# Attention step of a one-core hybrid layer: order of transposes, scores and fillers on TensorE

## The chip, the core and the metric

The kernel runs on one core of one Trainium2 chip. The metric is the device time of one execution in microseconds (us). Before the change it is 689.45 us, the median of 3 runs (689.14 to 689.67).

## The reference

The layer computes, for 1024 tokens of width 1024 (batch 1, one layer, float32):

```python
u = layer_norm(x) * (1 + scale) + shift          # scale, shift, gate from silu(c) @ w_ada + b_ada
fq, fk, fv, fg, ff, sq, sk, sv, sg = split(u @ w_in)
# 8 heads of 64, forgetting attention: causal softmax of q k / 8 + f_cum[query] - f_cum[key]
# 8 heads of 64, stick-breaking: sigmoid(z) times the product of sigmoid(-z) over the later keys
y = concat([fox * silu(fg), stick * silu(sg)]) @ w_out
out = layer_norm(2 ** 0.25 * x + gate * y, ln_g, ln_b)
```

## The kernel before, in words

**Number format.** Most products are done in three matmuls of float32r: each operand is split into a rounded high part and a low rest, and high x high, low x high and high x low are accumulated in PSUM. `m_step` (L292) is one such triple for a block of 128 input rows and 512 tokens.

**Pairs and units.** The 16 heads are handled as 8 pairs p; pairs 0 to 3 are the stick-breaking heads, 4 to 7 the forgetting ones. A unit (p, h, i) is one head h of a pair and one block i of 128 queries, with (i+1)*128 keys. There are 128 units, in an order that `order` (L1010) gives: i rises for the first four pairs, falls for the next three, and the last pair goes by query blocks from the last to the first.

**The steps of a unit.**
- `att_scores` (L445): the score matmuls S (L457, L458) into the only score tile; then for the stick-breaking heads two sigmoids on ACT (L479, L481), a running product on DVE (L486, L490) and a product on POOL (L492); for the forgetting heads a sum with minimum on DVE (L465), an exponential on ACT (L470), a reciprocal on DVE (L471) and a scaling on POOL (L473). The DVE instruction L465 is ordered behind the latest low part of the transposes (the list `lows`).
- `att_query` (L426): ACT copies the next unit's query block (L431).
- `att_transpose` (L497): TensorE transposes the weights, 128 columns at a time, in groups of up to four into one of two PSUM tiles T (L509); ACT copies a group as the high part (L511), DVE makes the low part (L512). Once a pair of query blocks is complete, its value product `att_pv` (L519, matmuls L526) is issued after the first group of the next unit's transposes; ACT, DVE and POOL then form the gated output (L533 to L536), which goes to DRAM.

**Fillers.** The projections of later pairs are not a stage of their own. They are written as generators whose pieces (six matmuls as a rule, and some pieces without any) are put between the attention's instructions. `fill(want)` (L1005) runs pieces until a count is reached, and the list `want` spreads `FILL[p]` pieces over the 16 units of pair p in half steps. `gen_last_g` (L969) is the last filler: the gate projection of pair 7, on two accumulators, with a load of the output weights of one pair (`load_wo`, L845) after each piece. In pair 7 its pieces are spread over the first `G7` units. The accumulators have two buffers (tag acc). After that the output projection's pieces (`tail`, `o_step` L888) fill in, `TAIL` pieces per step, from unit 116 on.

**What sets the order.** TensorE's instructions run in the order in which the program writes them (a manual schedule from L138 to the end). The other engines' queues are ordered by a planner from the program; `after(...)` puts instructions behind named ones of the same engine. The softmax work of unit k has a lag of `LAG` = 2 steps: step k of the loop at L1036 issues the scores of unit k and the transposes of unit k-2. `HELD` names the steps at which parts of pair 0's projections, held in SBUF, are evacuated (`evac_m`, L313).

Step k of the loop before the change, on TensorE: scores of unit k; first filler piece; transposes of unit k-2 with the value product that is ready; second filler piece; output pieces where it is their turn.

Of the kernel before, what the change touches and what calls it, by code (L numbers as in the profile page):

```python
# [16 lines left out]
NB = 8  # L17
# [10 lines left out]
def tile_hybrid_layer(  # L28
# [30 lines left out]
    def pt_tile(name, dt=F32R, shape=None):  # L59
        return big("pt", 3, name, dt, shape or [P, 2, 1024])  # L60

    def acc_tile(name):
        return ps.tile([P, 512], F32, tag="acc", bufs=2, name=name)

    def pv_tile(name, which=0):
        return ps.tile([P, 512], F32, tag=f"pv{which}", bufs=1, name=name)

    def t_tile(name):
        return ps.tile([P, 512], F32, tag="T", bufs=2, name=name)
# [13 lines left out]
    def after(*instructions):  # L83
        stack = ExitStack()
        for i in instructions:
            stack.enter_context(tc.issue_after(i.ins))
        return stack
# [177 lines left out]
    def evac_q(p, ch, acc, qst, heads):  # L265
        s = slice(ch * 512, ch * 512 + 512)
        for h in heads:
            r = slice(h * HD, h * HD + HD)
            o = slice((1 - h) * HD, (1 - h) * HD + HD)
            nc.scalar.activation(qst[h][r, s], acc[r, :], AF.Copy, scale=SCALE)  # L270
            nc.vector.scalar_tensor_tensor(qst[h][o, s], acc[r, :], SCALE, qst[h].bitcast(F32)[r, s],
                                           op0=ALU.mult, op1=ALU.subtract)
# [14 lines left out]
    def evac_g(p, ch, acc, sg):  # L287
        s = slice(ch * 512, ch * 512 + 512)
        nc.scalar.activation(sg[:, s], acc, AF.Tanh, scale=0.5)
        nc.vector.scalar_tensor_tensor(sg[:, s], sg[:, s], 1.0, acc, op0=ALU.add, op1=ALU.mult)  # L290
# [22 lines left out]
    def evac_m(p, m, ch, acc, heads=(0, 1)):  # L313
        if m == 0:
            evac_q(p, ch, acc, qst[p], heads)
        elif m == 1:
            return evac_k(p, ch, acc, kst[p], klo[p], heads)
        else:
            evac_g(p, ch, acc, sgt[p])
# [113 lines left out]
    masks, scaled, lows = [], [], []  # L433

    def att_causal(u):
        p, h, i = u
        if p >= 4:
            if not masks:
                masks.append(pv_tile("causal_ps", 1)[:, :P])
                nc.vector.tensor_copy(masks[0], causal)  # L440
            f = fb[2 * (p - 4) + h]
            dg = slice(i * P, i * P + P)
            nc.vector.tensor_tensor(f[:, dg], f[:, dg], masks[0], op=ALU.add)
# [53 lines left out]
    def att_transpose(u, between=()):  # L497
        p, h, i = u
        a = st_w.pop(u)
        j, qo = i // 2, (i % 2) * P  # L500
        for g in range((i // 4) + 1):
            n = min(4, i + 1 - 4 * g)
            if (p, h, j, g) not in st_pt:
                st_pt[p, h, j, g] = pt_tile(f"pt_{p}_{h}_{j}_{g}", F32R, [P, 2, 4, 256])
            hi, lo = (st_pt[p, h, j, g][:, x] for x in range(2))
            tp = t_tile(f"T_{p}_{h}_{i}_{g}")
            for b in range(n):
                kb = 4 * g + b
                nc.tensor.transpose(tp[:, b * P:(b + 1) * P], a[:, kb * P:(kb + 1) * P], ident)  # L509
            t3 = tp[:, :n * P].rearrange("p (a b) -> p a b", a=n)  # L510
            nc.scalar.copy(hi[:, :n, qo:qo + P], t3)  # L511
            lows[:] = [nc.vector.tensor_tensor(lo[:, :n, qo:qo + P], t3, hi.bitcast(F32)[:, :n, qo:qo + P],  # L512
                                               op=ALU.subtract)]
            while between:
                att_pv(*between.pop(0))
# [281 lines left out]
    for kb in range(NB):  # L797
# [9 lines left out]
        if kb < len(evacs):  # L807
            n, h = evacs[kb]
# [4 lines left out]
    held = att_tile("st_held")  # L813
# [31 lines left out]
    def load_wo(pr):  # L845
        hi = big(f"u{pr}", 1, f"woh_{pr}", F32R)
        lo = big(f"v{pr}", 1, f"wol_{pr}", F32R)
        nc.sync.dma_start(hi.bitcast(F32), wo_dr[0, pr])
        nc.sync.dma_start(lo.bitcast(F32), wo_dr[1, pr])
        wo[pr] = (hi, lo)  # L850
# [118 lines left out]
    def gen_last_g(p):  # L969
        tiles = fetch_m(p, 2)  # L970
        yield
        make_g(p)
        accs = [acc_tile(f"m_{p}_2_{ch}") for ch in range(2)]
        for kt in range(NB):
            for ch in (1, 0):
                m_step(accs[ch], tiles, kt, ch)
            if kt == NB - 1:
                for ch in (1, 0):
                    evac_m(p, 2, ch, accs[ch])
            load_wo(kt)  # L980
            yield

    fillers = chain([
# [10 lines left out]
    LEAD = 2  # L994
    LAG = 2
    W0 = 100.0
    OUT0 = 4
    TAIL = (2, 2, 2, 2, 2, 2, 4, 4, 4, 4, 8)
    G7 = 6
    HELD = {4: (1, 1), 5: (0, 0), 6: (1, 0), 10: (0, 1)}  # L1000
    FIRST_UNITS = 5
    YLOAD = (6, 9, 12, 14, 16)
# [2 lines left out]
    def fill(want):  # L1005
        while done[0] < want:
            done[0] += 1
            next(fillers, None)
# [10 lines left out]
    units = [u for p in range(NPAIR) for u in order(p)]  # L1019
    want = [0.0]  # L1020
    for p in range(NPAIR):
# [3 lines left out]
        if p == NPAIR - 1:  # L1025
            size = [1] * G7 + [0] * (16 - G7)
        for w in size:
# [3 lines left out]
    seen = set()  # L1031
    ready = []
    LAST = 16 * (NPAIR - 1)
    tail = chain([gen_out_first(6), gen_out_last(6)] + [gen_out(t) for t in OUT_ORDER[1:]])
    fill(2)
    for k in range(len(units) + LAG + 1):  # L1036
        if k < len(units):
            if k == 16 * 4 - 1:
                load_fb(0)
                load_fb(1)  # L1040
            if k == 0:
                att_query(units[0])
            issued = att_scores(units[k], units[k + 1] if k + 1 < len(units) else None)
            if k == 16 * 4 - 1:
                att_causal(units[k + 1])
            if k + 1 < len(units):
                att_query(units[k + 1])
            p, h, i = units[k]
            if 4 <= p < NPAIR - 1 and i == 0:
                load_fb(2 * (p - 4) + h + 2)  # L1050
        fill(want[2 * k + LEAD + 1])
        if LAG <= k < len(units) + LAG:
            u = units[k - LAG]
            att_transpose(u, ready)
            if k in HELD:
                m, h = HELD[k]
                with after(*issued, *lows):
                    evac_m(0, m, 1, held[:, m * 512:(m + 1) * 512], (h,))
            seen.add(u)
            if (u[0], u[1], u[2] ^ 1) in seen:  # L1060
                ready.append((u[0], u[1], u[2] // 2))
        while k >= len(units) + LAG and ready:
            att_pv(*ready.pop(0))
        fill(want[2 * k + LEAD + 2])
        if k >= LAST + OUT0:
            for _ in range(TAIL[min(k - LAST - OUT0, len(TAIL) - 1)]):
                next(tail, None)
        if k == LAST:
            load_y(6)
            load_ln()  # L1070
        for i, d in enumerate(YLOAD):
            if k == LAST + d:
                load_y(OUT_ORDER[i + 1])
# [64 lines left out]
```

## Time and profile before

| what | value |
|---|---|
| median of 3 runs | 689.45 us (689.14 to 689.67) |
| profiled execution, its own time | 689.13 us |
| its span, first to last instruction | 687.2 us |
| TensorE matmul busy | 671.8 us |
| mean granted TensorE clock | 0.997 |
| VectorE (DVE), ScalarE (ACT), GpSimd (POOL) busy | 488.3, 381.3, 403.2 us |
| packets' time on the DMA queue of most transfers | 33.8% of 16 engines' span |

The profile is one execution of the program. Times of its rows count from the span's start. PE is TensorE, PEld its weight loads, SP the engine that issues most DMAs. In a timeline row stand the start, the duration, the engine, the line, the operation, output and inputs by name, the shape and a count; in brackets the idle time of the engine before it and what ended it. The ends of matmuls are modelled.

### The profile page before, as it was taken

To read this page: it belongs to the slowest core of one execution; us is meant where nothing else is said; L and a number is where in the kernel's file an instruction comes from. 1 tells how busy PE (TensorE), PEld (TensorE's weight loads), DVE (VectorE), ACT (ScalarE), POOL (GpSimd) and SP (SyncE) were. 2 spreads that over 40 slices of the span, in tenths; PEclk is the share of its full clock that TensorE was granted. 3 is DMA by queue.
4 is the path that set the end of the run, shared out by engine and by line. 5 is a ranking of instruction groups with operands and counts; after the bars stand their busy time and mean duration, and the time that the engine had idled before them with its cause. 6 is when DMAs were issued, how large, how long until landed. Compare 5 with 4: busy or idle time off the path is not lost.

```text
span 687.2 us, 11196 instructions
## 1 busy us (share of the span) xinstructions
PE 671.8 (98%) x3709; PEld 571.2 (83%) x3709; DVE 488.3 (71%) x996; ACT 381.3 (55%) x857; POOL 403.2 (59%) x529
## 2 busy tenths in 40 slices
PE   8999999999999999999999999999999999999995
PEld 5788888788998888889988888889988878888885
DVE  6696769968668677777776675766676778785645
ACT  6566377756667666566665564655565666521000
POOL 5650179746447655556369878668785365655411
PEclk9999999999999999999999999999999999999998
DMA  9954422112102112112134455254352297143301
GB/s 335 409 221 170 152 74 76 40 26 55 40 9 70 40 54 55 40 50 58 36 104 128 161 162 166 80 176 146 116 163 72 60 353 300 59 174 106 118 31 61
DMA packets 45272, 81.54 MB, mean 119 GB/s; under 512 B 5216, under 2 KB 19360, under 8 KB 44960
## 3 DMA queue, kind: packets, MB, share of 16 engines
q1 hardware_dynamic: 43632, 76.54, 33.8%
q10 hardware_dynamic: 1584, 4.31, 1.9%
q8 instruction: 29, 0.48, 0.3%
q14 instruction: 27, 0.22, 0.1%
HBM read 60.34 MB, written 16.29 MB: 112 GB/s over the span
## 4 chain that ended last, share of the span: by engine, by line
PE 83%; DVE 6%; DMA 4%; ACT 3%; POOL 2%; issue 2%; DVEq 0%; POOLq 0%; ACTq 0%
PE m L296 9%; PE pv L526 9%; PE m L298 9%; PE m L297 9%; PE T L509 9%; PE S L458 4%; PE S L457 4%; PE o L901 4%; PE o L900 4%; PE o L899 4%; PE v L354 3%; PE v L352 3%; PE v L353 3%; DMA wss<-in_w_ss_dram 3%; PE st_late L612 1%
## 5 line engine op out<-in xcount | busy, mean ns | idle before, releaser
L296 PE MATMUL m<-uh,whi 128*128 128x512 f32 x304 | 125.0, 411 | 0.7 <-DVE kl L284 0.7
L512 DVE TENSOR_TENSOR pt<-T,pt 128x512 fp32r<-128x512 f32 (+2 forms) x192 | 103.1, 551 | 26.0 <-ACT pt L511 24.2
L298 PE MATMUL m<-uh,wlo 128*128 128x512 f32 x304 | 119.7, 394 | 0.0
L297 PE MATMUL m<-ul,whi 128*128 128x512 f32 x304 | 119.6, 394 | 0.0
L511 ACT CAST pt<-T 128x512 fp32r<-128x512 f32 (+2 forms) x192 | 88.6, 478 | 42.0 <-PE T L509 39.1
L492 POOL TENSOR_TENSOR be<-be,kp 128x127 f32<-128x127 f32 (+3 forms) x64 | 77.1, 1204 | 37.2 <-DVE kp L490 27.6
L486 DVE TENSOR_TENSOR_SCAN kp<-kp,floor 128x512 f32<-128x512 f32 (+2 forms) x64 | 65.1, 1018 | 27.6 <-ACT kp L479 25.4
L526 PE MATMUL pv<-pt,v 128*128 128x512 f32 x320 | 82.8, 388 | 0.3 <-DVE pt L512 0.3
L536 POOL TENSOR_TENSOR ty<-ty,sg 64x256 f32<-64x256 f32 x64 | 47.0, 734 | 42.6 <-DVE ty L535 18.3
L473 POOL TENSOR_SCALAR a<-a,l 128x1024 f32<-128x1024 f32 (+3 forms) x64 | 48.2, 752 | 39.7 <-DVE l L471 29.5
L298 PEld LDWEIGHTS m<-uh,wlo 128*128 128x128 f32 x304 | 57.1, 188 | 13.7
L457 PE MATMUL S<-k,q 128*128 128x512 f32 (+5 forms) x192 | 66.2, 346 | 0.2 <-DVE nm L465 0.2
L296 PEld LDWEIGHTS m<-uh,whi 128*128 128x128 f32 x304 | 57.2, 188 | 10.1 <-DVE kl L284 1.1
L458 PE MATMUL S<-kl,qz 128*128 128x512 f32 (+5 forms) x192 | 65.3, 341 | 0.0
L470 ACT ACTIVATE a<-a,nm 128x1024 f32<-128x1024 f32 (+3 forms) x64 | 49.8, 778 | 26.4 <-DVE nm L465 25.8
L297 PEld LDWEIGHTS m<-ul,whi 128*128 128x128 f32 x304 | 57.3, 189 | 7.9
L526 PEld LDWEIGHTS pv<-pt,v 128*128 128x128 f32 x320 | 55.4, 189 | 9.6 <-DVE pt L512 0.6
L479 ACT ACTIVATE kp<-S 128x128 f32<-128x128 f32 (+3 forms) x64 | 41.8, 652 | 33.7 <-PE S L458 31.3
L465 DVE CUSTOM_DVE_ANT_0 a<-S,fb 128x1024 f32<-128x1024 f32 (+3 forms) x64 | 48.2, 754 | 15.8 <-PE S L458 12.4
L431 ACT CAST qz<-q 64x128 fp32r<-64x128 f32 x128 | 37.3, 295 | 34.5 <-PE S L458 33.3
L352 PE MATMUL v<-whi_v,uh 128*128 128x256 f32 (+1 forms) x192 | 55.5, 289 | 0.0
L354 PE MATMUL v<-wlo_v,uh 128*128 128x256 f32 (+1 forms) x192 | 54.3, 283 | 0.3 <-POOL wlo_v L127 0.3
(290 smaller groups left out, 1625.0 us busy)
## 6 DMA issues: line engine op xcount, KB each, us to landing
raw<-in_w_qkg_dram SPq DMA_DIRECT2D x38, 256.0 KB, 2.6
wss<-in_w_ss_dram SPq DMA_DIRECT2D x12, 512.0 KB, 8.4
x<-in_x_dram SPq DMA_DIRECT2D x8, 512.0 KB, 6.8
k<-k SPq DMA_DIRECT2D x32, 128.0 KB, 2.3
wg<-in_w_gate_dram SPq DMA_DIRECT2D x8, 512.0 KB, 4.2
raw_o<-in_w_out_dram SPq DMA_DIRECT2D x16, 256.0 KB, 3.0
fb<-f_dr ACTq DMA_DIRECT2D x8, 512.0 KB, 4.2
wo_dr<-whi_o SPq DMA_DIRECT2D x16, 256.0 KB, 2.2
```

The costliest lines, as they stand in the source:

```text
L296: nc.tensor.matmul(acc, hi[:, c], u_hi[kt][:, s], start=(kt == 0), stop=False)
L297: nc.tensor.matmul(acc, hi[:, c], u_lo[kt][:, s], start=False, stop=False)
L298: nc.tensor.matmul(acc, lo[:, c], u_hi[kt][:, s], start=False, stop=(kt == NB - 1))
L352: nc.tensor.matmul(acc[:, :n], u_hi[kt][:, ts_], hi[:, s], start=(kt == 0), stop=False)
L354: nc.tensor.matmul(acc[:, :n], u_hi[kt][:, ts_], lo[:, s], start=False, stop=(kt == NB - 1))
L457: nc.tensor.matmul(S[:, s, :w], qst[p][h][:, qs], kst[p][h][:, ks], start=True, stop=False)
L458: nc.tensor.matmul(S[:, s, :w], z, klo[p][:, ks], start=False, stop=True)
L486: last_dve = nc.vector.tensor_tensor_scan(rv, rv, floor[:, :ke - lo], initial=0.0, op0=ALU.mult, op1=ALU.max)
L492: nc.gpsimd.tensor_tensor(be[:, :ke - 1], be[:, :ke - 1], kp[:, 1:ke], op=ALU.mult)
L511: nc.scalar.copy(hi[:, :n, qo:qo + P], t3)
L512: lows[:] = [nc.vector.tensor_tensor(lo[:, :n, qo:qo + P], t3, hi.bitcast(F32)[:, :n, qo:qo + P], op=ALU.subtract)]
L526: nc.tensor.matmul(acc2[:, :, q0:], vt[p][:, kb, h * P:(h + 1) * P], pt[:, :, q0:], start=(kb == 0), stop=(kb == last))
```

## The change

In each step the transposes with the value product come first, then the scores, then both filler pieces together. The held evacuations come right behind the scores' reads instead of behind the transposes' low parts. In the last gate projection the first two pieces are each two blocks of input rows for one accumulator (first that of the upper 512 tokens, then that of the lower), where before each piece was one block for both; later pieces are as before. Its pieces are spread over 5 units instead of 6.

```diff
@@ gen_last_g
-        accs = [acc_tile(f"m_{p}_2_{ch}") for ch in range(2)]
-        for kt in range(NB):
-            for ch in (1, 0):
+        accs = {ch: acc_tile(f"m_{p}_2_{ch}") for ch in (1, 0)}
+        for n in range(NB):
+            for kt, ch in ([(0, 1 - n), (1, 1 - n)] if n < 2 else [(n, 1), (n, 0)]):
                 m_step(accs[ch], tiles, kt, ch)
-            if kt == NB - 1:
+            if n == NB - 1:
                 for ch in (1, 0):
                     evac_m(p, 2, ch, accs[ch])
-            load_wo(kt)
+            load_wo(n)
             yield
@@ constants
-    G7 = 6
+    G7 = 5
@@ the loop over steps
     for k in range(len(units) + LAG + 1):
+        if LAG <= k < len(units) + LAG:
+            u = units[k - LAG]
+            att_transpose(u, ready)
+            seen.add(u)
+            if (u[0], u[1], u[2] ^ 1) in seen:
+                ready.append((u[0], u[1], u[2] // 2))
+        while k >= len(units) + LAG and ready:
+            att_pv(*ready.pop(0))
         if k < len(units):
...
             issued = att_scores(units[k], units[k + 1] if k + 1 < len(units) else None)
             if k == 16 * 4 - 1:
                 att_causal(units[k + 1])
+            if k in HELD:
+                m, h = HELD[k]
+                with after(*issued):
+                    evac_m(0, m, 1, held[:, m * 512:(m + 1) * 512], (h,))
             if k + 1 < len(units):
                 att_query(units[k + 1])
...
-        fill(want[2 * k + LEAD + 1])
-        if LAG <= k < len(units) + LAG:
-            u = units[k - LAG]
-            att_transpose(u, ready)
-            if k in HELD:
-                m, h = HELD[k]
-                with after(*issued, *lows):
-                    evac_m(0, m, 1, held[:, m * 512:(m + 1) * 512], (h,))
-            seen.add(u)
-            if (u[0], u[1], u[2] ^ 1) in seen:
-                ready.append((u[0], u[1], u[2] // 2))
-        while k >= len(units) + LAG and ready:
-            att_pv(*ready.pop(0))
         fill(want[2 * k + LEAD + 2])
```

## The prediction

> **What bounds the kernel now.** I read the profile's page first, for the share of TensorE and its clock.
>
> ```profile
> span 687.2 us, 11196 instructions
> ...
> PE 671.8 (98%) x3709; PEld 571.2 (83%) x3709; DVE 488.3 (71%) x996; ACT 381.3 (55%) x857; POOL 403.2 (59%) x529
> ...
> PEclk9999999999999999999999999999999999999998
> ```
>
> TensorE is busy for 98% of the span at nearly full clock, and the change neither adds nor removes a matmul. So the time can only move by the places where TensorE stands still, and by new ones. The second view is therefore the waits of TensorE from 82 us, where the attention steps begin, to 630 us, where the last scores and value products are done: who it waited for, us in total, times, longest.
>
> ```profile
> PE T L509 <- DVE pt L512: 1.7, 3, 1.4
> PE m L296 <- DVE kl L284: 0.7, 1, 0.7
> PE T L509 <- POOL be L492: 0.4, 1, 0.4
> PE pv L526 <- DVE pt L512: 0.3, 1, 0.3
> PE v L354 <- POOL wlo_v L127: 0.3, 1, 0.3
> PE S L457 <- DVE nm L465: 0.2, 1, 0.2
> ```
>
> This is all there is to win. The v line is a weight cast on POOL that the change leaves where it is. The other seven waits sum to 1.7+0.7+0.4+0.3+0.2 = 3.3 us. The third view is the timeline around the longest one, engine by engine (start, duration, engine, line).
>
> ```profile
> 118.64 0.82 PE L509 MATMUL T<-ident,be 128*128 128x128 f32 x6
> ...
> 122.67 0.39 PE L298 MATMUL m<-uh,wlo 128*128 128x512 f32 x1
> 124.42 0.63 PE L509 MATMUL T<-ident,be 128*128 128x128 f32 x4 [1.35 <-DVE pt L512]
> ```
>
> ```profile
> 119.76 1.02 ACT L481 ACTIVATE be<-S 128x1024 f32<-128x1024 f32 x1
> ...
> 121.01 0.84 ACT L511 CAST pt<-T 128x512 fp32r<-128x512 f32 x2
> ```
>
> ```profile
> 123.60 1.00 DVE L512 TENSOR_TENSOR pt<-T,pt 128x512 fp32r<-128x512 f32 x2
> ```
>
> Unit 9's transposes are issued by 119.2 us, but ACT copies them at 121.01 only, because the scores of step 11 were issued before them and ACT works through these (until 120.78) first. DVE's low parts follow at 123.60, behind its scans. Unit 10's transposes need the same two PSUM tiles and wait. The row says 1.35 us idle. From issue to issue it is 124.42 - 122.67 = 1.75 us where one such matmul follows another after 0.23 us (509.71 to 509.95, below, is 0.24), so the loss is 1.52. The page says that ends of matmuls are modelled: a matmul stands there with 0.39 us and the next one follows after 0.23, so 0.16 us per stall is hidden. Seven waits then cost 3.3 + 7 x 0.16 = **4.4 us**.
>
> **The change part by part.** I number units and steps k from 0; step k holds the scores of unit k and the transposes of unit k-2. I call the transposes with the value product between them the bundle.
>
> *1. The bundle goes ahead of the scores (removes waits).* ACT and DVE then meet the copies of a bundle before the scores of the same step, not behind 2 us of score reads. That is the cause in the row above, and I take the T waits (1.7 and 0.4), the pv wait and the S wait as gone. Their worth, with the hidden part, is 2.6 + 6 x 0.16 = 3.6 us. The bounds are 0 (the copies turn out late for another reason) and 3.6. I take 3.6, because the copy is always the younger of the two after the change.
>
> *2. The last gate projection starts with six matmuls on one accumulator.*
>
> ```profile
> 552.22 0.50 PE L296 MATMUL m<-uh,whi 128*128 128x512 f32 x1 [0.68 <-DVE kl L284]
> ```
>
> ```profile
> 551.47 0.69 DVE L284 TENSOR_TENSOR kl<-m,k 64x512 fp32r<-64x512 f32 x1 [0.15 <-ACT k L279]
> ```
>
> Today three matmuls run and then the second accumulator is needed, which DVE still reads until 552.16. With six, the second one is needed 3 x 0.23 = 0.7 us later, and by part 1 a bundle lies ahead of it as well. This removes 0.68 + 0.16 = 0.8 us. The cover is the three extra matmuls; without them the 0.8 stays. Its load of output weights for pair 0 now waits for the second piece, about 1.4 us later on SP's queue, with y stores and loads behind it; the first product that uses them comes some 20 us later, so it costs nothing.
>
> *3. Transposes lose lead.* Before, unit k's transposes came after the scores of step k+2 and one filler piece. After, they come where those scores now begin, while unit k's own scores come later by the bundle of unit k-2. The softmax chain in between ends with POOL's scaling. The tightest unit is 100.
>
> ```profile
> 509.71 0.40 PE L458 MATMUL S<-kl,qz 128*128 128x512 f32 x1
> 509.95 0.60 PE L509 MATMUL T<-ident,a 128*128 128x128 f32 x4
> ...
> 512.28 0.42 PE L457 MATMUL S<-k,q 128*128 128x384 f32 x1
> ...
> 514.11 0.71 PE L509 MATMUL T<-ident,a 128*128 128x128 f32 x5
> 514.58 0.48 PE L296 MATMUL m<-uh,whi 128*128 128x512 f32 x1
> ...
> 516.06 0.28 PE L457 MATMUL S<-k,q 128*128 128x256 f32 x1
> ```
>
> ```profile
> 510.25 0.69 DVE L465 CUSTOM_DVE_ANT_0 a<-S,fb 128x512 f32<-128x512 f32 x1 [0.29 <-issue]
> ```
>
> ```profile
> 515.24 0.70 POOL L473 TENSOR_SCALAR a<-a,l 128x512 f32<-128x512 f32 x1
> ```
>
> POOL ends at 515.94 and the new place of the transposes is that of the scores at 516.06, so 0.12 us are left, if POOL's end doesn't move. What POOL does just before (weight casts) doesn't depend on the scores, so I take it as not moving. The bound on the other side is that it moves by the whole bundle, 512.28 - 509.95 = 2.33 us; that is the first rival. Three more units are as tight:
>
> ```profile
> 458.81 0.38 PE L509 MATMUL T<-ident,a 128*128 128x128 f32 x2
> ...
> 459.85 0.29 PE L352 MATMUL v<-whi_v,uh 128*128 128x256 f32 x1
> ...
> 465.56 0.34 PE L457 MATMUL S<-k,q 128*128 128x384 f32 x1
> ```
>
> ```profile
> 464.34 1.12 POOL L473 TENSOR_SCALAR a<-a,l 128x1024 f32<-128x1024 f32 x1
> ...
> 499.37 1.12 POOL L473 TENSOR_SCALAR a<-a,l 128x1024 f32<-128x1024 f32 x1
> ```
>
> ```profile
> 494.46 0.38 PE L509 MATMUL T<-ident,a 128*128 128x128 f32 x2
> ...
> 495.50 0.40 PE L296 MATMUL m<-uh,whi 128*128 128x512 f32 x1
> ...
> 500.62 0.33 PE L457 MATMUL S<-k,q 128*128 128x384 f32 x1
> ```
>
> ```profile
> 109.34 0.49 PE L509 MATMUL T<-ident,be 128*128 128x128 f32 x3
> ...
> 110.02 0.33 PE L457 MATMUL S<-k,q 128*128 128x384 f32 x1
> ...
> 112.63 0.47 PE L457 MATMUL S<-k,q 128*128 128x448 f32 x1
> ```
>
> ```profile
> 111.34 1.31 POOL L492 TENSOR_TENSOR be<-be,kp 128x639 f32<-128x639 f32 x1
> ```
>
> Unit 88 has 465.56 - 465.46 = 0.10 left, unit 96 500.62 - 500.49 = 0.13, unit 8 112.63 - 112.65 = -0.02. Four places within 0.15 us of waiting won't all hold. I allow **0.7 us**, an estimate: at each of the four the chain may be late by a third of one low part on DVE (two take 1.00 us above, so 0.17 each). The bounds are 0 and the first rival's 4.7.
>
> *4. Two scores come too close together.* In step 100 no filler matmul is issued (512.28 follows the bundle directly). Today the bundle of unit 98 lies between scores 100 and 101; after, only that of unit 99, 514.58 - 514.11 = 0.47 us. Scores 100 end at 510.11 and DVE has read them at 510.94, which is 0.83 later, and there is one score tile. Scores 101 would start 0.47 less the hidden 0.16 after that end, so TensorE waits 0.83 - 0.31 = 0.5 us, with every filler and transpose queued behind. Step 110 is alike:
>
> ```profile
> 548.62 0.28 PE L458 MATMUL S<-kl,qz 128*128 128x256 f32 x1
> ```
>
> ```profile
> 549.03 0.42 DVE L465 CUSTOM_DVE_ANT_0 a<-S,fb 128x256 f32<-128x256 f32 x1 [0.34 <-issue]
> ```
>
> Scores end at 548.90, are read at 549.45, and three transposes (three fifths of 0.47) lie between: 0.55 - 0.12 = 0.4 us. Against it stands nothing; DVE is told to do the bundle's low part before it reads, so it can only be later. I add 0.5 + 0.4 + 0.3 for that order = **1.2 us**, bounds 0.9 and 2.
>
> *5. The rest costs nothing.* Fillers in one piece are the same matmuls. The held evacuations move ahead of the next query copy on ACT and DVE; the scores that need that copy are a whole step away. G7 = 5 gives step 112 a second piece (1.4 us more for unit 112's chain) and takes it from step 116, where output products already fill. If that cover is short, step 118 waits a few tenths, inside the allowance.
>
> **Sum.** Removed 3.6 + 0.8 = 4.4; added 0.7 + 1.2 = 1.9; net -2.5 us. The profiled execution took 689.13 (span 687.2 and 1.9 around it) and would take 686.6. It lies 0.3 below the median 689.45, so I forecast **687.0**. About 0.2% (1.4 us) is what a measurement of this kernel can tell from no change.
>
> **Rivals.** *A. Slower: POOL follows the scores.* If POOL's scaling is bound to the scores, it moves by the bundle, and the four units wait 2.33 - 0.12 = 2.2, 1.04 - 0.10 = 0.9, 1.04 - 0.13 = 0.9 and 0.68 + 0.02 = 0.7 us, together 4.7. With 1.9 added and 4.4 removed that is +2.2: **691.7**. It decides from the point where POOL's end passes the start of scores k+2. For it speaks that the slack is near zero at all four; against it that POOL was in the middle of weight casts there.
>
> *B. No change.* The copies come early, but two or three of those units wait 0.9 each: 2.5 more, **689.5**. The same rows speak for it.
>
> *C. The clock.* The granted clock is lower where TensorE has gaps:
>
> ```profile
> 626.00:687.00 61.00, 54.09 (x255) 44.65 (x253) 32.31 (x54) 1.56 (x4) 18.80 (x24) 0.96 0.22 79
> ```
>
> There it is 0.96 (the seventh number), in the steps 9 tenths or more by the page's row. If the new order brought the steps from 82 to 626 us to 0.96, they would take 544 x 0.04 = 22 us more, **709**. What speaks against it is that the order doesn't lengthen a run of transposes: at most eight, 8 x 0.1 us, before the scores. The Trainium skill, TensorE: Matmul & The Clock Gate, section "Part 4: PE-mode transpose", says that transposes do not count as TensorE activity for the clock in the way matmuls do, a rule that speaks against gathering transposes; the trace's row of clock shows no dip in the steps as they are, eight transposes in a run included.
>
> *D. Part 2 does nothing* because DVE's read moves too: 0.8 less gained, **687.8**.
>
> **How the numbers follow.** Forecast 0.47, A 0.25, B 0.22, C 0.02, D 0.04. Faster by over 0.2% (below 688.1): forecast and D, 0.51. Within: B, 0.22. Slower (above 690.8): A and C, 0.27. The forecast's own range is 685.0 (nothing added) to 688.0. The range that should hold the time 8 times in 10 goes from 684.8 to 692.0, which takes in A and B and leaves out C and the far sides.
>
> **What would show it.** Right: no wait of T on L512 over 0.2 us; no wait on L284 near 552; two new waits of S L457 on DVE L465 of about half a us, at units 101 and 111; ACT's copies L511 directly behind their transposes. Wrong: waits of T on POOL L473 or L492 that sum to over 2 us (A, B), a clock row below 9 in the steps (C), or a wait on L284 still there (D). The forecast fails if the planner, which orders ACT, DVE and POOL anew, puts casts ahead of the scalings.

## The result and the profile after

The changed kernel takes 694.46 us, median of 6 runs (692.81 to 696.03), against 689.62 us (689.14 to 690.61) for the kernel before in the same session. The ratio is 1.0066, 95% interval 1.0049 to 1.0083: 0.66% slower. The profiled execution took 694.85 us with a span of 693.1; before it was 689.13 and 687.2. So the profile has to account for 5.9 us. From the page of the changed kernel, the same lines as before:

```profile
span 693.1 us, 11208 instructions
...
PE 674.0 (97%) x3709; PEld 573.1 (83%) x3709; DVE 484.5 (70%) x996; ACT 380.6 (55%) x857; POOL 406.5 (59%) x529
...
PEclk9999999999999999999999999999999999999999
```

TensorE does the same 3709 matmuls, and the row of clock shows no dip in 40 slices of 17 us. The mean granted clock is 0.995, where it was 0.997. Both means take in the end of the program, where TensorE has done its last matmul and the clock stands at 0.50 (from 682.4 us on before, from 690.2 after), so they say little about the steps; the windows below do. The waits of TensorE from 82 to 640 us, after (who waits for whom: us in total, times, longest):

```profile
PE T L509 <- POOL a L473: 4.4, 6, 2.0
PE T L509 <- POOL be L492: 1.5, 1, 1.5
PE S L457 <- DVE nm L465: 0.9, 2, 0.6
PE v L354 <- POOL wlo_v L127: 0.9, 1, 0.9
```

Everything that the change was to remove is gone: no wait on L512, none on L284, and the old wait of S, at unit 106, is gone too (the two of the row above are new, at units 101 and 107). In its place stand 5.9 us of transposes that wait for POOL, where there were 0.4. What the removal looks like, on ACT at 119 us (the place of the longest wait before):

```profile
119.45 0.86 ACT L511 CAST pt<-T 128x512 fp32r<-128x512 f32 x2
120.53 1.03 ACT L479 ACTIVATE kp<-S 128x1024 f32<-128x1024 f32 x1 [0.21 <-PE S L458]
```

The copies of the transposes now stand ahead of the score reads, 1.56 us earlier than the 121.01 of before.

**An account by steps.** For every unit I took the start of its score matmuls after the change, less the start before, less the time of the bundle that has moved ahead of them. What is left is how far TensorE is behind (plus) or ahead (minus). All steps of 0.4 us or more in absolute value, and smaller ones where the table says so:

```
at the scores of     change   what the trace shows there (after)
unit 6                -0.58   the old wait of 0.30 of a value product is gone; -0.85 in total by then
unit 10               +1.75   T of unit 8 waits 1.46 for POOL L492
unit 13               -1.60   the old wait of 1.35 is gone
units 25, 33, 41      -1.31   (0.39, 0.61, 0.31) old waits of 0.21, 0.44 and 0.16 are gone
                              1.8 us ahead from unit 49 to unit 81
unit 82               +1.46   T of unit 80 waits 1.23 for POOL L473
unit 89               +0.73   v waits 0.86 for its cast L127
unit 100              +3.48   T of unit 98 waits 2.00 for POOL L473, and low clock
unit 101              +1.00   S waits 0.28 for the score tile
unit 107              +1.25   T waits 0.27, S waits 0.63 for the score tile
unit 111              +0.53   two scores close together, T waits 0.18
unit 112              -0.92   the old wait on L284 is gone
units 113 to 117      +0.2    fillers of the last gate projection, shifted
unit 118              +0.73   T waits 0.50 for POOL L473
end                   +6.0
```

From unit 13 to unit 81 the kernel is ahead, in the end by 1.8 us; it loses from unit 82 to unit 111. The gains stand in the steps where the old waits stood.

**The three waits on POOL.** POOL's rows around unit 98 (start, duration, line; in brackets its own idle time and what ended it), after:

```profile
503.72 1.02 POOL L473 TENSOR_SCALAR a<-a,l 128x896 f32<-128x896 f32 x1
507.36 0.62 POOL L126 TENSOR_SCALAR whi<-raw 128x512 fp32r<-128x512 f32 x1 [2.62 <-DMA raw<-in_w_qkg_dram]
508.06 1.33 POOL L127 TENSOR_TENSOR wlo<-raw,whi 128x512 fp32r<-128x512 f32 x1
509.47 0.73 POOL L536 TENSOR_TENSOR ty<-ty,sg 64x256 f32<-64x256 f32 x1
510.28 0.62 POOL L126 TENSOR_SCALAR whi<-raw 128x512 fp32r<-128x512 f32 x1
510.88 0.91 POOL L473 TENSOR_SCALAR a<-a,l 128x768 f32<-128x768 f32 x1
```

The last of them in the kernel before:

```profile
507.28 0.90 POOL L473 TENSOR_SCALAR a<-a,l 128x768 f32<-128x768 f32 x1
```

The scaling of unit 98 (the row of 128x768) starts 3.6 us later than before, 510.88 against 507.28. Its input was ready long before that:

```profile
506.10 0.16 DVE L471 RECIPROCAL l<-l 128x1 f32<-128x1 f32 x1 [0.32 <-ACT a L470]
```

From 506.26 to 510.88 it stood in POOL's queue behind three rows of weight casts, the first of which waited for its load (2.62 us of idle time on POOL), and a gated output. Before the change the same unit's reciprocal was done at 503.84, and the scaling stood in the queue for 3.44 us, behind a cast that waited 1.13 us for its load. So of the 3.6 us, 2.4 are an input that is ready later (its scores come 1.4 us later, and DVE reads them behind the bundle's low parts, at 504.05 instead of 501.61), and 1.2 a longer stand in the queue. What sets the time of the scaling is the queue, which comes free last. By the trace, the loads were late because the casts before them were. There are two raw buffers, which the output weights use as well; POOL's casts L127 from them end at 502.46 and 503.74, and SP issues the next loads right behind:

```profile
502.87 0.42 SPq L122 DMA_DIRECT2D raw<-in_w_qkg_dram  x1
503.39 0.39 SPq L867 DMA_DIRECT2D lngb<-in_ln_g_dram  x1
503.88 0.37 SPq L122 DMA_DIRECT2D raw<-in_w_qkg_dram  x1
504.31 1.61 SPq L868 DMA_DIRECT2D lngb<-in_ln_b_dram  x1
```

Before, both weight loads were issued ahead of the two loads of the norm's weights (503.69 and 504.07):

```profile
499.79 2.32 SPq L122 DMA_DIRECT2D raw<-in_w_qkg_dram  x2
```

Now the two kinds alternate, and the first weight load took 4.35 us to land, where it took 2.71 before. At unit 80 POOL is later by only 0.5 us. The scaling before the change:

```profile
427.85 1.14 POOL L473 TENSOR_SCALAR a<-a,l 128x1024 f32<-128x1024 f32 x1
```

After it, with TensorE 1.8 us earlier:

```profile
428.39 2.11 POOL L473 TENSOR_SCALAR a<-a,l 128x1024 f32<-128x1024 f32 x2
...
429.56 0.66 PE L509 MATMUL T<-ident,a 128*128 128x128 f32 x4 [1.23 <-POOL a L473]
```

**The clock after the longest wait.** The waiting transposes of unit 98 and what follows, on TensorE:

```profile
511.84 0.66 PE L509 MATMUL T<-ident,a 128*128 128x128 f32 x4 [2.00 <-POOL a L473]
512.25 3.15 PE L526 MATMUL pv<-pt,v 128*128 128x512 f32 x8
515.20 0.63 PE L509 MATMUL T<-ident,a 128*128 128x128 f32 x2
```

```profile
511.80:514.00 2.20, 2.16 (x9) 1.83 (x10) 0.69 (x1) 0.59 (x1) 2.20 (x3) 0.71 0.04 11
514.00:516.00 2.00, 2.00 (x7) 1.67 (x7) 0.12 (x1) 0.45 (x2) 1.89 (x3) 0.50 0.48 131
516.00:518.00 2.00, 1.72 (x10) 1.27 (x9) 1.97 (x6) 1.63 (x5) 1.88 (x3) 0.96 0.59 130
```

In the windows (start and end, length, busy time of five engines, then the granted clock, DMA share and GB/s) the clock falls to 0.71 and 0.50; in the 2 us before them it was 1.00. The eight value products take 515.20 - 512.25 = 2.95 us up to the next transpose, where eight at the usual 0.23 would take 1.8. At half clock this is 2.2 x 0.29 + 2.0 x 0.50 + 2.0 x 0.04 = 1.7 us of clock lost, so some 3.4 us at one half. In finer windows the clock falls at 512.7, 0.9 us after TensorE has started again, and is back at 516.1, so the work behind the wait pays. A slice of the page is 17 us and hides it. Of the 3.48 us lost at unit 100, 2.0 + 0.16 are the wait and 1.3 the clock.

### The profile page after: what moved, and what is told of

It is laid out like the page before. It is cut to its first block, busy times and chain, and to the rows that moved or that the text cites. A ratio compares the mean times of both kernels' runs of the same rounds, so it can differ in the third digit from the quotient of the medians.

```text
span 693.1 us, 11208 instructions
## 1 busy us (share of the span) xinstructions
PE 674.0 (97%) x3709; PEld 573.1 (83%) x3709; DVE 484.5 (70%) x996; ACT 380.6 (55%) x857; POOL 406.5 (59%) x529
## 4 chain that ended last, share of the span: by engine, by line
PE 79%; DMA 7%; POOL 4%; DVE 4%; issue 3%; ACT 2%; SPq 0%; POOLq 0%; DVEq 0%; ACTq 0%
PE pv L526 9%; PE m L296 8%; PE m L297 8%; PE m L298 8%; PE T L509 8%; PE o L901 4%; PE o L899 4%; PE o L900 4%; PE S L457 4%; PE S L458 4%; PE v L354 4%; PE v L352 4%; PE v L353 4%; DMA raws<-in_w_v_dram 1%; DMA raws<-in_w_qkg_dram 1%
## 5 line engine op out<-in xcount | busy, mean ns | idle before, releaser
L512 DVE TENSOR_TENSOR pt<-T,pt 128x512 fp32r<-128x512 f32 (+2 forms) x192 | 103.8, 552 | 55.1 <-ACT pt L511 53.7
L511 ACT CAST pt<-T 128x512 fp32r<-128x512 f32 (+2 forms) x192 | 88.9, 479 | 69.4 <-PE T L509 67.8
L296 PE MATMUL m<-uh,whi 128*128 128x512 f32 x304 | 120.6, 397 | 0.0
L457 PE MATMUL S<-k,q 128*128 128x512 f32 (+5 forms) x192 | 73.1, 382 | 0.9 <-DVE nm L465 0.9
L353 PE MATMUL v<-whi_v,ul 128*128 128x256 f32 (+1 forms) x192 | 54.1, 282 | 0.0
L465 DVE CUSTOM_DVE_ANT_0 a<-S,fb 128x1024 f32<-128x1024 f32 (+3 forms) x64 | 48.0, 750 | 3.1 <-PE S L458 1.8
L127 POOL TENSOR_TENSOR wlo<-raw,whi 128x512 fp32r<-128x512 f32 x38 | 49.2, 1297 | 1.1
```

The source lines that it names most:

```text
L296: nc.tensor.matmul(acc, hi[:, c], u_hi[kt][:, s], start=(kt == 0), stop=False)
L353: nc.tensor.matmul(acc[:, :n], u_lo[kt][:, ts_], hi[:, s], start=False, stop=False)
L457: nc.tensor.matmul(S[:, s, :w], qst[p][h][:, qs], kst[p][h][:, ks], start=True, stop=False)
```

## The experiments

Each run was timed in five rounds beside the kernel before. My theory **P** was that the new order shortens the lead of a unit's scores over its transposes, and that POOL's scaling, in a queue with weight casts, doesn't fit in where POOL is loaded. Beside it stood **S** (the score tile is read late), **C** (the clock), **D** (the norm loads hold up the weight loads), and the rival **Q**, that the order itself is the loss, in every step.

The loop was cut by steps in four runs, with this edit (shortened, with comments added; the condition differs; "old order" is that of the kernel before):

```diff
+    def ahead(k):
+        return k < 80        # or 11 <= k < 80, 11 <= k < 100, k >= 80
     for k in range(len(units) + LAG + 1):
+        if ahead(k):
+            transposes(k)    # bundle first, held evacuation behind the scores
...
+        if not ahead(k):
+            fill(want[2 * k + LEAD + 1])
+            transposes(k)    # old place, held evacuation behind it
         fill(want[2 * k + LEAD + 2])
```

**1. The last gate projection alone.** Old order and G7 = 6, new start of the accumulators (the first hunk of the diff).

> The old step order with the new start of the last gate projection (G7 stays 6). Theory P (the loss sits in the step order alone: transposes lost their lead and wait for POOL's scaling, which stands behind weight casts in POOL's queue): the wait on L284 near 552 us goes and nothing comes in its place, 0.5 to 0.9 us faster than before. Rival G (the gate projection's start shares in the loss): slower than before, with new waits after 550 us.

Measured: 688.7 us beside 689.33, ratio 0.9993 (0.9984 to 1.0001); profiled span 686.5 against 687.2. Its waits:

```profile
PE T L509 <- DVE pt L512: 1.8, 3, 1.4
PE v L354 <- POOL wlo_v L127: 0.6, 1, 0.6
```

No wait on L284 is left in the list, whose other rows stand as before but for 0.3 more on v. By the account the scores of unit 112 come 0.96 us earlier. The gain is real in the trace, and as a time just at the edge of what five rounds tell apart.

**2. New order in steps 0 to 79 only** (with the new gate start, G7 = 6).

> The new step order for steps 0 to 79 alone, the old one from step 80 on, with the new start of the last gate projection and G7 = 6. Theory P: the changed kernel stood 1.8 us ahead of the old one at step 80 and lost all of its time after it, where POOL casts the output weights as well. The lead should be kept: 1.5 to 2.8 us faster than before, no wait of a transpose on POOL after 420 us over 0.3 us. Rival Q (the new order loses wherever it is used, by DVE's reads that stand behind the low parts): slower than before or no gain, and the waits on POOL after 420 us come back in the old order.

Measured: 687.92 us, ratio 0.998 (0.9971 to 0.9989), faster by 1.4, just under the 1.5 expected at least. Its waits:

```profile
PE T L509 <- POOL be L492: 1.5, 1, 1.5
PE v L354 <- POOL wlo_v L127: 0.4, 1, 0.4
```

The first row is unit 8. No other transpose waits on POOL, and nothing else waits but S, once, 0.2. This speaks against Q: the same order gains for 80 steps. The loss belongs to steps 80 to 111.

**3. New order from step 80 on** (G7 = 5).

> The new step order from step 80 on alone, the old one before it, with the new start of the last gate projection and G7 = 5. Theory P: most of the loss, but less than the 7.8 us that the changed kernel lost after step 80, because TensorE arrives at step 80 some 1.8 us later and POOL has that much more time: the waits of transposes on POOL's scaling at units 80 and 98 shrink by up to 1.8 us each; 1 to 5 us slower than before. Rival Q: the waits don't shrink, since they come from the order within a step: 6 us or more slower than before.

Measured: 695.67 us, ratio 1.0096 (1.0082 to 1.0109), slower by 6.3, more than the 5 at most that P gave, and a time that Q had named (6 or more); the waits, though, shrink as P had it.

```profile
PE pv L526 <- DVE pt L512: 1.6, 2, 1.3
```

One part of it is a cost of the cut: at step 80 the bundle of unit 78 follows the one of unit 77 at once, and the value product waits 1.33 us. The wait of unit 80 vanishes here, since TensorE has no lead of 1.8 us to lose, while unit 98 still waits 1.16. From unit 82 on this kernel loses 5.0 us, the changed kernel 6.3. So the lead won earlier explains unit 80 and a part of unit 98, and not the rest.

**4. All scalings on DVE.**

```diff
-                         nc.gpsimd.tensor_scalar(a[:, :ke], a[:, :ke], l, 1.0, op0=ALU.mult, op1=ALU.mult)]
+                         nc.vector.tensor_scalar(a[:, :ke], a[:, :ke], l, 1.0, op0=ALU.mult, op1=ALU.mult)]
```

> The changed kernel with the scaling of the forgetting heads (L473) on DVE instead of POOL. Theory P: the scaling no longer stands behind POOL's casts; the waits of transposes on L473 (4.4 us in six) go, and with them the stretch of half clock after the longest: 4 to 8 us faster than the changed kernel, at or under the time before. Rival Q (the chain is late before it reaches POOL): waits of the same size on DVE's scaling, under 2 us gained.

Measured: 692.07 us, ratio 1.0042 (1.0029 to 1.0054), 2.4 below the changed kernel, where I expected 4 to 8.

```profile
PE T L509 <- DVE a L473: 2.3, 3, 1.2
```

POOL's scalings were the wait in pairs 5 and 6: without them on POOL no transpose waits for a scaling until 554 us, and the clock shows no dip there. But the three waits of this row stand behind that, at the end of pair 6 and in pair 7, where DVE becomes the late one.

**5. The norm loads behind the last weight load.**

```diff
-        nc.sync.dma_start(raw, src)
+        weight_load[:] = [nc.sync.dma_start(raw, src)]
...
-            load_ln()
+            with after(*weight_load):
+                load_ln()
```

> The changed kernel with the loads of the last norm's gain and bias (two of 512 KB) ordered on SP behind the last weight load. In the changed kernel they were issued at 503.4 and 504.3 us, between and beside two weight loads, which took 4.3 us to land where 2.7 is the rule; POOL stood 2.62 us in a cast that waited for one of them, with unit 98's scaling behind it. Theory D (that collision makes the longest wait): unit 98's wait falls from 2.0 to 0.8 us or less, the half clock after it goes, 2 to 3.5 us faster than the changed kernel (about 691.5). Rival P (POOL's casts alone are the backlog): the wait stays over 1.5 us and the gain under 1 us.

Measured: 693.67 us, ratio 1.007 (1.0056 to 1.0084), 0.8 below the changed kernel instead of 2 to 3.5; the two intervals overlap, so the time alone doesn't tell it from no change. (In this run and in runs 7, 9 and 12 the line numbers are two higher: L511 is the transposes' line and L475 the scaling.)

```profile
511.69 0.66 PE L511 MATMUL T<-ident,a 128*128 128x128 f32 x4 [0.94 <-POOL a L475]
```

The wait of unit 98 is halved and the clock stays at 1.00 in all windows from 509.8 to 522 us, but POOL's cast ahead of it still waits 1.75 us, until 507.17. The wait alone says too much for D: these transposes start only 0.15 us earlier than in the changed kernel (511.69, not 511.84), and TensorE came to the place 0.9 later in this execution. POOL was 0.7 later as well when the weight load was issued (503.54, not 502.87), and the load landed in 3.49 us, not 4.35; so D is worth some 0.8 us here. By the trace D is a part, and not the main one.

**6. Two matmuls into a spare score tile ahead of step 100's bundle**, to fill the wait. They add work and leave the result alone.

```diff
+        if k == 100:
+            busy(2, s_tile("warm")[:, 0, :])
         if LAG <= k < len(units) + LAG:
```

> The changed kernel with two matmuls of float32 identity, 512 columns, that belong to no result, on TensorE ahead of the bundle of step 100, where it waits 2.0 us for POOL. Theory C (the wait also costs by the clock, which the trace shows at 0.71 and 0.50 in the 4 us behind it): the wait is filled, the clock stays at full, the eight value products go back from 0.43 to 0.23 us apart, 1 to 2 us faster than the changed kernel. Rival (the clock falls for another reason, or the products are slow by themselves): no change or up to 1 us slower by the added work.

Measured: 693.45 us, ratio 1.0058 (1.0045 to 1.0071), 1.0 below the changed kernel, again with intervals that overlap. The rows of the spare matmuls and of unit 98's transposes:

```profile
510.59 1.88 PE L176 MATMUL warm<-ident 128*128 128x512 f32 x4
...
512.78 0.66 PE L509 MATMUL T<-ident,a 128*128 128x128 f32 x4 [0.31 <-POOL a L473]
```

The clock stays at 1.00. This run came to step 100 later than the changed kernel's profile (its last filler matmul ahead of the step starts at 510.36, not 509.44), yet the span ends 0.3 earlier, so from there on it is 1.2 us shorter. POOL's scaling was late by as much as in the changed kernel, so this is not a shorter wait. It agrees with the 1.3 us put on the clock.

**7. A filler piece held back from steps 99, 105 and 109 to the next**, on top of run 5, to part the close scores.

```diff
-        fill(want[2 * k + LEAD + 2])
+        fill(want[2 * k + LEAD + 2] - (k in (99, 105, 109)))
```

> The kernel of the moved norm loads, and in steps 99, 105 and 109 one filler piece less, which then falls into the next step, whose own piece has no matmuls. Theory S (in those steps two scores stand too close for the one score tile): the waits of S on L465 at units 101, 107 and 111 go, which cost 1.0, 1.2 and 0.5 us by the distance of scores to those of before; 1.5 to 2.7 us faster than with the norm loads moved alone. Rival: the transposes of those steps, which then come a piece earlier, wait for POOL by as much; no gain.

Measured: 697.04 us, ratio 1.011 (1.0096 to 1.0124), the slowest of all. The waits on the score tile are gone, as S has it, but:

```profile
PE T L511 <- POOL a L475: 5.4, 4, 2.6
PE T L511 <- POOL be L494: 1.5, 1, 1.5
PE S L459 <- DMA k<-k: 1.2, 1, 1.2
PE m L298 <- DVE kl L286: 1.1, 1, 1.1
```

Six matmuls fewer in a step are 1.4 us less lead for the next transposes. The wait of unit 98 is 2.59 us, and the clock dips again behind it:

```profile
512.00:514.00 2.00, 2.00 (x9) 1.58 (x8) 0.69 (x1) 0.59 (x1) 2.00 (x4) 0.68 0.10 33
514.00:516.00 2.00, 2.00 (x8) 1.71 (x7) 0.76 (x2) 0.74 (x2) 1.26 (x2) 0.50 0.26 98
```

**8. New order in steps 11 to 79** (new gate start, G7 = 6): the old order where unit 8 waited.

> The new step order in steps 11 to 79 alone, the old one before and after, with the new start of the last gate projection and G7 = 6. The new order in steps 0 to 79 measured 687.92; its trace has a wait of 1.46 us of unit 8's transposes on POOL, which the old order doesn't have, and the old order's wait of 1.4 at unit 10 comes from copies that step 11 decides. Theory P: both go, 1.2 to 2 us faster than with steps 0 to 79, about 686.4. Rival: the old wait at unit 10 comes back, no gain.

Measured: 687.7 us, ratio 0.9974 (0.9966 to 0.9983): faster than both kernels, by 1.9 than the one before, but only 0.2 below run 2, where 1.2 to 2 were expected. The wait of unit 8 is gone, but where the order switches, units 11 and 12 lose 0.67 and 0.52 by the account, and a wait of S on DVE, 1.19 us at unit 114, has come.

**9. Scalings of pairs 4 to 6 on DVE, those of pair 7 on POOL, and the norm loads later** (runs 4 and 5 together, with DVE only where `p < NPAIR - 1`).

> The changed kernel with the scalings of pairs 4 to 6 on DVE (pair 7's stay on POOL) and the two norm loads behind the last weight load. Theory P (the scalings wait in POOL's queue behind weight casts): the waits of T on POOL at units 80 and 98 (1.2 and 2.0 us) and the clock's dip go, and in pair 7 DVE has no scalings to be late with; the waits of S on the score tile at units 101, 107 and 111 stay (about 1.2 us together) and the wait of v on its cast stays (0.9): 3 to 5 us below the changed kernel, 689.5 to 691.5. Rival Q (the new order makes DVE late by itself, and every load on DVE adds to it): waits on DVE at units 98 to 111 take the place, 692 or more, no better than with all scalings on DVE.

Measured: 690.19 us, ratio 1.0008 (0.9999 to 1.0017): 4.3 below the changed kernel, in the middle of what P gave.

```profile
PE T L511 <- POOL be L494: 1.4, 1, 1.4
PE S L459 <- DVE nm L467: 1.1, 4, 0.3
PE T L511 <- DVE pt L514: 0.8, 2, 0.6
```

The waits of units 80 and 98 on POOL, the dip of the clock and the wait of v are gone. This is the strongest run for P.

**10. New order in steps 11 to 99.**

> The new order in steps 11 to 99, the old order before and from step 100 on, and the new start of the last gate projection over 6 units. If the loss of the changed kernel after step 80 lies at unit 80 (scaling on POOL, 1.5), at the cast of v (0.6 more) and in steps 100 to 111 (scores too close, the late scaling of unit 98), this kernel pays only the first two, 2 us, and keeps the 3 us gained before: 688.0 to 690.0. If the new order costs a little at every step of pairs 5 and 6, it is 690.5 or more.

Measured: 690.76 us, ratio 1.002 (1.001 to 1.003), with a wide spread (689.64 to 692.74); so by its time it belongs to the second case (690.5 or more). The profiled execution, one of the faster ones (689.81), shows what the first case named: +1.63 at unit 82 (unit 80 waits 1.41 on POOL), +1.22 at unit 89 (v), +0.50 at unit 101, and nothing else from step 80 to 99. So the steps are those of the first case, priced too low (3.35 us, not 2), and the 1 us between the profiled execution and the median stays unexplained. Adding twenty steps to run 8 costs 3 us.

**11. DVE's score read ordered as before.** In the changed kernel the list `lows` at L465 holds the low parts of the same step's bundle, since that now comes first. Here it holds those of the step before.

```diff
-            with after(*lows):
+            with after(*older):
                 nc.vector.tensor_tensor_reduce(out=v3(a), in0=S[:, :ns, :w], in1=v3(f),
...
     def att_transpose(u, between=()):
+        older[:] = lows
```

> The changed kernel with one edit: DVE's read of the scores (L465) is ordered behind the last low part of the step before, as it stood before the change, and no longer behind the low parts of the same step's transposes, which now come ahead of the scores. Theory S (the score tile comes free late because DVE does the bundle's low part before it reads): the waits of S on L465 at units 101 and 107 (0.28 and 0.63 us) go and with them the losses at units 101, 107 and 111 (1.0, 1.25 and 0.5), while the waits on POOL at units 8, 80 and 98 stay: 1.5 to 2.7 us below the changed kernel, 691.8 to 693.0. Rival (the scores merely stand too close on TensorE, whatever DVE does first): the S waits stay, within 0.5 us of the changed kernel, 694 to 695; or the low parts that now come later make transposes wait as much.

Measured: 693.5 us, ratio 1.0057 (1.0043 to 1.007), 1.0 below the changed kernel, less than the 1.5 of theory S and more than the rival's 0.5, with intervals that overlap; what tells the two apart is the trace. DVE around the read for unit 106 in the changed kernel:

```profile
538.62 0.41 DVE L534 TENSOR_TENSOR ty<-pv,ty 64x256 f32<-64x256 f32 x1 [0.23 <-ACT ty L533]
539.24 0.69 DVE L512 TENSOR_TENSOR pt<-T,pt 128x512 fp32r<-128x512 f32 x1 [0.20 <-ACT pt L511]
539.84 0.41 DVE L535 TENSOR_TENSOR ty<-pv,ty 64x256 f32<-64x256 f32 x1
540.17 0.94 DVE L465 CUSTOM_DVE_ANT_0 a<-S,fb 128x768 f32<-128x768 f32 x1
```

The scores start at 536.96, and the read is done 4.16 us later, behind two low parts and two steps of the gated output, all of the bundle. In run 11 the scores start at 534.91 and the read (536.00, its last part until 536.96) is done 2.05 us later. The waits of S at units 101 and 107 are gone: theory S is shown for these waits, but not for the time that they were to give back. By the account units 107 and 111 still lose 1.07 and 0.54; what is saved, 2.0 us, lies at units 100 to 102: the transposes of unit 98 no longer wait, those of units 99 and 100 wait 1.38 and 0.68 for POOL instead, and the clock stays at 1.00. But the transposes of unit 105, next in line, now wait 0.95 on POOL: the reciprocal of that unit, ready at 536.16, stands behind the read on DVE until 536.88, and POOL scales from 537.15 on. The waits moved to POOL:

```profile
PE T L509 <- POOL a L473: 5.0, 5, 1.4
```

**12. All of it together:** new order from step 11, G7 = 5, the edits of runs 9 and 11.

> All causes taken out at once: new order from step 11 on (no wait of unit 8), scalings of pairs 4 to 6 on DVE, norm loads behind the last weight load, score reads ordered as in the kernel before. If the causes are these and add up: 690.2 (the run with the scalings on DVE and later norm loads) less 1.5 for unit 8 and about 1 for the reads, 687.0 to 688.5. If they don't add up, because DVE is late with scalings and low parts wherever the reads come first: 689 or more, no better than the kernel before.

Measured: 691.3 us, ratio 1.0031 (1.0021 to 1.0042). The causes don't add up; the case I called the second holds.

```profile
PE T L511 <- DVE a L475: 2.3, 2, 1.8
```

The longest, 1.85 us at 535.88, is again the scaling ahead of unit 105's transposes, this time on DVE behind a read and a low part. In both orders tried on DVE, something of that chain is late in pair 6.

## Why the prediction was wrong, point by point

The sign and the range were wrong: forecast 687.0, range up to 692.0, measured 694.46.

**1. The bundle ahead of the scores: right.** Forecast 3.6 us. The waits on L512 and the old one of S are gone, and the gains of the account up to unit 41 are 0.85 + 1.60 + 1.31 = 3.8, less 0.3 given back at unit 8: 3.5.

**2. The last gate start: right.** Forecast 0.8; 0.92 at unit 112, and 0.96 in run 1.

**3. Transposes lose lead: this is the step that failed.** "What POOL does just before (weight casts) doesn't depend on the scores, so I take it as not moving", and an allowance of 0.7 us. Measured are 1.75 (unit 8), 1.46 (unit 80), 3.48 (unit 98, its 1.3 of low clock included) and 0.73 (unit 118, which point 5 had put at a few tenths), 7.4 us, and 0.73 more at the cast for v, which I had left out as unmoved. Three things were wrong in it.

First, the slack was read against the start of the scores before, but step 1 itself moves TensorE ahead by 1.8 us, and an engine that stays in place is late by that much. At unit 80 the scaling ended before the change at 427.85 + 1.14 = 428.99, and scores 82 stood here:

```profile
429.95 0.34 PE L457 MATMUL S<-k,q 128*128 128x384 f32 x1
```

That is a slack of 0.96, so I didn't list it; 1.8 of lead and 0.5 on POOL less that slack make 1.3 of the 1.46 us lost there. A lead can be kept only as far as the first place whose pace something else sets.

Second, POOL does move. At unit 98 the scaling is 3.6 us later. Its input follows the scores, as rival A had it for POOL (ready 2.4 us later); and the queue ahead of it is later too, by a cast that comes later, a load that is issued later for it, and a cast ahead of the scaling that waits for that load. I had ended the forecast with the planner putting casts ahead of the scalings, yet at this place they stood ahead in both orders; it was the late load that turned a harmless order into a stop.

Third, I looked for tight places one by one instead of asking how far the lead shrinks everywhere. Median time from a unit's first score matmul to its first transpose, by pair, in us:

```
pair      0     1     2     3     4     5     6     7
before   8.9  11.3  10.9  10.9  11.1  11.2   9.4   8.1
after    6.4   8.1   7.9   7.8   7.7   8.0   7.5   7.1
```

Some 3 us are gone in pairs 1 to 5. In pairs 1 to 4 what is left is enough (run 2 has no such wait there); in 5 and 6, where POOL is busier and some steps hold few fillers, it isn't. POOL's share (the fifth busy time) is 229.48 of 347 us, 66%, up to unit 80, and 60.45 of 83 us, 73%, behind it. In the windows of the changed kernel:

```profile
82.00:429.00 347.00, 344.77 (x1981) 299.71 (x1979) 252.66 (x473) 222.91 (x504) 229.48 (x295) 1.00 0.25 71
429.00:512.00 83.00, 79.58 (x498) 71.05 (x499) 53.44 (x144) 45.33 (x116) 60.45 (x69) 1.00 0.45 139
```

Units 88, 96 and 100, which I had named as the tightest, don't wait at all: TensorE had been stopped at 80, at the cast for v and at 98 just before.

**4. Scores too close: the mechanism right, the size and one place not.** Forecast 1.2 us at units 101 and 111; these steps lost 1.00 + 1.25 + 0.53 = 2.8 at three (units 101, 107, 111). The waits of S, with the hidden part, are 0.44 + 0.79 = 1.2 of that, at 101 and 107; that this equals the forecast is luck, since unit 107 wasn't in it. The rest is mostly transposes that wait for POOL in the same steps and, at unit 101, the last of the low clock. "DVE is told to do the bundle's low part before it reads, so it can only be later" was the right thought, with 0.3 us for it. Run 11 shows how late: without that order the read for unit 106 is done 2.1 us earlier after its scores.

**5. The rest: right** but for the shift in the last gate projection, which comes to 0.2.

**The rivals.** A, POOL following the scores, gave 691.7 and was the nearest. It put 4.7 us of waits on POOL; 5.9 came, but mostly at units 8, 80 and 98, and none at 88, 96 and 100. C looked for a lower clock in runs of transposes over all steps; the clock fell elsewhere, behind one long wait, and for 3.4 us only. Its row of 0.96 was misread: up to 682 us all windows of that row show 1.00, and the rest is the end of the program, with TensorE done at 680.1. None of the rivals had waits and clock together, so the range ended too low.

**What is shown and what is not.** That the loss lies in steps 80 to 111 and not in the order as such is shown by runs 2 and 8. That the waits on POOL's scalings and the clock behind them are the larger part is shown by run 9 (4.3 us back with its two edits, the intervals well apart), that score reads wait behind the bundle's work by run 11. Run 9 makes two edits at once; each alone gave less (2.4 in run 4, 0.8 in run 5), so how the 4.3 divide is not shown. The shares of the norm loads (0.8) and of the clock (about 1.2) rest on the traces of one run each, since the medians differ by less than their intervals. Not settled is how to have the new order in pairs 5 and 6 at no loss: run 12 took out every cause by name and still lost 0.3%. A third raw weight buffer, which would set the loads free from the casts, wasn't tried.

## What to carry to other kernels

Before an operation is moved ahead of its producer's neighbours, list for every stage how long its input needs through all queues, and compare that with the lead that is left, counting the lead that the change itself wins: gained time is spent at the first engine that keeps its own pace. A queue that mixes ready work with casts that wait for loads turns a late load into a stop for everyone. An order that helps in some stages and hurts in others can be switched by stage: steps 11 to 79 alone make 0.26% faster what costs 0.66% over all of them.

## What the runs showed of the hardware that was not expected

Behind a wait of TensorE of 2.00 us its granted clock fell to one half for about 3.4 us, and behind one of 2.59 us in run 7 it did the same (0.68, 0.50, then 0.97 in windows of 2 us). With the wait filled (run 6) it did not fall. The price was some 1.2 us beside the wait. No shorter wait in the steps lowered it: after the 1.46 us at 113.73 the windows stay at 1.00, and so they do after 1.85 us in run 12.

```profile
113.00:115.00 2.00, 1.27 (x8) 1.14 (x9) 1.14 (x2) 0.58 (x1) 2.00 (x4) 1.00 0.12 33
```

```profile
535.88 0.95 PE L511 MATMUL T<-ident,a 128*128 128x128 f32 x7 [1.85 <-DVE a L475]
```

Whether 2 us is a threshold isn't shown. In the traces the level holds for whole multiples of 3.413 us (here 505.17 us, 148 times that, then 3.41 at one half, then 174.08, 51 times that; 675.84, 198 times, in the kernel before), so where in such a step a wait falls may count as much as its length; no run separates the two.

The Trainium skill, TensorE: Matmul & The Clock Gate, section "Part 1: The HAM clock gate (the "warmup" mystery)", puts the drop to half clock after an idle window of about 3.4 us, and the return after about 3.4 us of work. The level (0.50) and the time to return agree with the trace; the idle time doesn't, since 2.0 us was enough here. Its section "Part 4: PE-mode transpose" doesn't count transposes as activity, which would stretch the gap to 512.25 - 509.84 = 2.4 us, still short of 3.4. In run 12 the stretch without a matmul other than transposes is longer, 536.59 - 534.03 = 2.56 us, and the clock stays at 1.00, so that length alone doesn't decide here either.
